# Query, output and down projections of a hybrid attention block, turned to row-wise weights and token-major results

## The chip, the cores and the metric

The kernel runs on one core of a Trainium2 chip. The metric is the device time of one launch in microseconds (us), weights read from HBM and the result written back to it. The core's engines are TensorE (PE; its weight loads are shown apart as PEld), VectorE (DVE), ScalarE (ACT), GpSimd (POOL) and SyncE (SP), which only issues transfers. All arithmetic is float32. A product is made to float32 precision from halves: each operand is split into a high part, rounded to the format fp32r that PE reads at full rate, and a low part, the rest; of the four products of halves three are added up.

## The reference

16 meta tokens go ahead of 256 tokens of 1024 channels, so L = 272. Cut to what matters here:

```python
a = rmsnorm(h, norm_mix_g)
q, k, v, qi, ki, wi, cu, cb, cc, ga, gb = split(a @ w_in)      # qi: 8 indexer heads of 64
y_attn = dsa_attention(q, k, v, qi, ki, wi) @ w_attn_out       # indexer scores -> top-k keys -> softmax
y_conv = (cb * short_conv(cc * cu, conv_w)) @ w_conv_out
h = h + (sigmoid(ga) * y_attn + sigmoid(gb) * y_conv) @ w_out
f = rmsnorm(h, norm_ffn_g)
h = h + (silu(f @ w_gate) * (f @ w_up)) @ w_down               # d_ff = 2816
out = rmsnorm(h, norm_final_g)[:, 16:]
```

## The kernel before

All activations lie channel-major: 128 channels on the partitions, tokens along the free dimension, 8 such tiles for 1024 channels. A weight matrix is cut into units of 128 x 1024 (512 KB). In a unit of the projections lie the eight 128 x 128 blocks that give 128 output channels. The list `UNITS` sets the order of all 158: four units of indexer queries (`qi`), three early gates, indexer keys (`ki`), convolution, attention, gates and branch outputs, eight of `wo`, 44 of gate and up, 22 of down. w0, w1, ... below are units by their place in that list. SP loads them in this order into seven buffers (`load_to`, line 130), ACT makes the high half (line 137), DVE the low half (line 145), some units ahead of PE (`ahead`).

PE takes the weight block as stationary operand and the activations as moving operand. `product` (lines 250, 253) needs two matmuls per block: the high weights against the high and low activations side by side (512 columns), the low weights against the high ones (256 columns). `narrow` (lines 214 to 216) needs three of 256 to 272 columns.

**Opening.** SP loads the first weight unit and the activations `h_in` in turn (lines 169, 171). The query units w0 to w3 and the early gates run on activations that carry the gain but not yet the 1/rms (`uT`, made by ACT in line 544 and DVE in line 545), one unit after the other. In between ACT squares the eight tiles of h (line 554), DVE and POOL add them up, 12 small matmuls against a column of ones sum over channels (line 191), POOL raises to the power -1/2 (line 201) and PE spreads the result (line 207), ACT copies it to `rstd` (line 590). Then POOL, ACT and DVE make the normalised activations `aT`, tile by tile (lines 563 to 565), on which unit 7 (`ki`) and all later ones run. `indexer_queries` (lines 294, 296) moves each query unit out of PSUM, in two ACT and two DVE instructions, while the next one runs.

**Joint and end.** Each of the eight `wo` units gives 128 channels of the residual; DVE adds them to h, ACT and DVE make the two halves of the FFN's input `fT` (lines 633, 634) and ACT the squares, POOL adds these. The first gate unit follows, then eight small matmuls for the sums. Gate and up run in pairs for each 128 channels of d_ff. In the down part one output tile takes 22 blocks in a row in one PSUM bank. After the last one come transposes back to token-major (line 691), the sums, the power, four evictions with the scale (lines 702, 703) and four transfers out (line 705).

Of the kernel before, what the change touches and what calls it, by code (L numbers as in the profile page):

```python
# [11 lines left out]
F32 = mybir.dt.float32  # L12
# [4 lines left out]
P = 128  # L17
# [25 lines left out]
START = [("w", 0, 4), ("h", 0, 2), ("h", 2, 4), ("w", 4, 8), ("h", 4, 6), ("h", 6, 8)]  # L43
# [22 lines left out]
LEAD = 4 + len(EARLY_GATES)  # L66


def program(nc, tc, h_in, params, weights, out):
# [94 lines left out]
    par = one.tile([P, 6 * KT], F32, name="par")  # L164
    nc.scalar.dma_start(par, params)
    raw[0] = raws.tile([P, D], F32, name="raw")
    for what, a, b in START:
        if what == "w":
            nc.sync.dma_start(raw[0][:, a * P:b * P], weights[0, :, a * P:b * P])
        else:  # L170
            nc.sync.dma_start(h_all[:, a:b], h_in[:, a:b])
    state["dma"] = 1
# [3 lines left out]
    g_mix, g_ffn, g_fin = (par[:, i * KT:i * KT + KT] for i in range(3))  # L176
    cw = par[:, 3 * KT:6 * KT]
# [9 lines left out]
    def token_sums(parts, groups, where=bank):  # L187
        o = [where() for _ in groups]
        for i, sq in enumerate(parts):
            for t, (c0, n) in enumerate(groups):  # L190
                mm(o[t][0:n, 0:1], sq[:, c0:c0 + n], ones, start=i == 0, stop=i == len(parts) - 1)
        return o

    def inverse_rms(o, groups):
        r = ring.tile([P, 3], F32, name="rt")
        if len(groups) == 3:
            V.memset(r[:, 0:1], 1.0)
        for t, (c0, n) in enumerate(groups):
            V.tensor_scalar(r[0:n, t:t + 1], o[t][0:n, 0:1], 1.0 / D, EPS, op0=OP.mult, op1=OP.add)
        r = r[:, 0:len(groups)]  # L200
        G.tensor_tensor(r, r, half[:, 0:len(groups)], OP.pow)  # L201
        return r

    def spread(r, groups):
        o = side()
# [12 lines left out]
    def narrow(i, src, c0=0, late=False):  # L218
# [4 lines left out]
        for k in range(KT):  # L223
            xh, xl = src.hi[:, k, c0:n], src.lo[:, k, c0:n]
            if late:
                mm(o, hi[:, w(k)], xh, start=k == 0, stop=False)
                mm(o, hi[:, w(k)], xl, start=False, stop=False)
            else:
                three_passes(o, hi[:, w(k)], lo[:, w(k)], xh, xl, k == 0, k == KT - 1)
        if late:  # L230
            for k in range(KT):
                mm(o, lo[:, w(k)], src.hi[:, k, c0:n], start=False, stop=k == KT - 1)
# [4 lines left out]

    def accumulate(h, o):
        V.tensor_tensor(h, h, o[:, 0:S], OP.add)  # L239
        if o.shape[1] > S:  # L240
            V.tensor_tensor(h, h, o[:, S:2 * S], OP.add)
# [12 lines left out]

    def product(i, src, c0=0):
        o = bank()
        hi, lo = got.pop(i)
        w = lambda k: slice(k * P, k * P + P)
        for k in range(KT - 1):
            wide_high(o, hi[:, w(k)], src, k, c0, start=k == 0, stop=False)  # L260
            wide_low(o, lo[:, w(k)], src, k, c0, start=False, stop=False)
        k = KT - 1
        wide_low(o, lo[:, w(k)], src, k, c0, start=False, stop=False)
        wide_high(o, hi[:, w(k)], src, k, c0, start=False, stop=True)
        return o

# [24 lines left out]
    def indexer_queries(o, j):  # L291
        rows = [(slice(e * DI, e * DI + DI), slice(DI - e * DI, P - e * DI)) for e in range(2)]
        for e, (mine, other) in enumerate(rows):
            act(qi[mine, 2 * j + e], o[mine], AF.Copy)
# [460 lines left out]
```

## Time and profile before

| | before |
|---|---|
| median of three runs | 499.12 us (498.91 to 499.23) |
| the profiled execution, its own time | 498.63 us |
| its span in the profile | 496.8 us |
| mean granted clock of PE | 0.996 |
| busy: PE, PEld, DVE, ACT, POOL | 487.0, 442.7, 362.3, 300.3, 73.4 us |
| transfers | 86.09 MB, mean 173 GB/s |

A busy PE is not PE at its peak, since matmuls overlap in the pipe: the step from one start to the next says more than the duration. The profile names lines of the kernel before; a helper's instructions all carry the helper's line.

### The profile page before, as it was taken

The page shows a single profiled execution, that of the slowest core. Times are in us where ns is not written, and L with a number is a line of the kernel's source. Part 1 is how long each engine was busy: PE and PEld are TensorE (multiplying, and loading weights), DVE is VectorE, ACT ScalarE, POOL GpSimd, SP SyncE. Part 2 cuts the span into 40 slices and gives each one's busy share as a digit, 9 for nine tenths or more (in the row PEclk, how much of TensorE's full clock was granted, in tenths as well). Part 3 has the DMA queues.
Part 4 walks back from the last instruction along what each step waited for, and adds up shares of the span by engine and source line. Part 5 has one row for each costly group of instructions (what it writes and reads, how often), then busy time and mean ns, then how long its engine had stood idle before and what let it go on. Part 6 is the DMA issues. An engine that isn't in the chain of part 4 may idle for free.

```text
span 496.8 us, 8349 instructions
## 1 busy us (share of the span) xinstructions
PE 487.0 (98%) x3157; PEld 442.7 (89%) x3157; DVE 362.3 (73%) x661; ACT 300.3 (60%) x567; POOL 73.4 (15%) x75
## 2 busy tenths in 40 slices
PE   8999999999999999999999999999999999999995
PEld 6989999999999999888888989888888888888895
DVE  4898888987777766787677796788777777664521
ACT  6685656665777776855555566566566565553511
POOL 3451113130000000000000022212211122001110
PEclk9999999999999999999999999999999999999998
DMA  8947446456443445365555465466555555655002
GB/s 304 331 136 254 136 162 206 154 194 212 149 148 128 147 155 162 102 198 181 202 188 194 136 233 184 136 205 211 178 202 172 190 192 178 219 195 171 1 0 86
DMA packets 24376, 86.09 MB, mean 173 GB/s; under 512 B 2832, under 2 KB 2832, under 8 KB 24336
## 3 DMA queue, kind: packets, MB, share of 16 engines
q1 hardware_dynamic: 24192, 85.54, 52.2%
q8 instruction: 25, 0.41, 0.4%
q14 instruction: 15, 0.12, 0.1%
q10 hardware_dynamic: 144, 0.02, 0.0%
HBM read 84.50 MB, written 1.05 MB: 172 GB/s over the span
## 4 chain that ended last, share of the span: by engine, by line
PE 90%; issue 3%; DVE 2%; ACT 1%; DMA 1%; POOL 1%; SPq 0%; POOLq 0%; DVEq 0%
PE acc L250 42%; PE acc L253 22%; PE acc L215 7%; PE acc L216 7%; PE acc L214 7%; DMA h_all<-in_h_in_dram 1%; DVE aT L565 1%; PE misc L409 1%; ACT temp L554 0%; PE misc L426 0%; PE misc L302 0%; POOL rt L201 0%; PE misc L214 0%; ACT whi L137 0%; PE misc L216 0%
## 5 line engine op out<-in xcount | busy, mean ns | idle before, releaser
L250 PE MATMUL acc<-aT,whi 128*128 128x512 f32 x576 | 202.5, 398 | 0.0
L145 DVE TENSOR_TENSOR wlo<-raw,whi 128x1024 fp32r<-128x1024 f32 x158 | 192.8, 1225 | 7.3 <-ACT whi L137 5.0
L137 ACT ACTIVATE whi<-raw 128x1024 fp32r<-128x1024 f32 x158 | 163.9, 1047 | 0.4 <-PE acc L250 0.3
L253 PE MATMUL acc<-aT,wlo 128*128 128x256 f32 x576 | 150.1, 281 | 0.0
L250 PEld LDWEIGHTS acc<-aT,whi 128*128 128x128 f32 x576 | 105.4, 188 | 19.3
L250 PE MATMUL acc<-big,whi 128*128 128x512 f32 x330 | 115.2, 394 | 0.0
L253 PEld LDWEIGHTS acc<-aT,wlo 128*128 128x128 f32 x576 | 108.9, 189 | 5.7
L253 PE MATMUL acc<-big,wlo 128*128 128x256 f32 x330 | 88.4, 282 | 0.0
L215 PE MATMUL acc<-aT,whi 128*128 128x272 f32 (+2 forms) x272 | 78.1, 287 | 1.1 <-DVE aT L565 1.1
L214 PE MATMUL acc<-aT,whi 128*128 128x272 f32 (+2 forms) x272 | 78.1, 287 | 0.0
L216 PE MATMUL acc<-aT,wlo 128*128 128x272 f32 (+2 forms) x272 | 77.6, 285 | 0.0
L246 DVE TENSOR_TENSOR temp<-acc,temp 128x256 f32<-128x256 f32 x87 | 36.9, 424 | 49.4 <-ACT temp L245 49.4
L250 PEld LDWEIGHTS acc<-big,whi 128*128 128x128 f32 x330 | 60.6, 188 | 11.9
L253 PEld LDWEIGHTS acc<-big,wlo 128*128 128x128 f32 x330 | 62.1, 188 | 2.5
L215 PEld LDWEIGHTS acc<-aT,whi 128*128 128x128 f32 x272 | 51.3, 189 | 1.8 <-DVE aT L565 1.3
L214 PEld LDWEIGHTS acc<-aT,whi 128*128 128x128 f32 x272 | 51.5, 189 | 0.1
L216 PEld LDWEIGHTS acc<-aT,wlo 128*128 128x128 f32 x272 | 51.2, 188 | 0.0
L119 ACT ACTIVATE big<-temp 128x256 fp32r<-128x256 f32 x45 | 18.8, 418 | 48.3 <-DVE temp L659 23.2
L622 POOL TENSOR_TENSOR sq_sum<-sq_sum,temp 128x256 f32<-128x256 f32 x12 | 11.0, 920 | 234.9 <-ACT temp L619 234.9
L245 ACT ACTIVATE temp<-acc 128x256 f32<-128x256 f32 x87 | 32.6, 375 | 13.8 <-PE acc L250 11.5
L655 POOL TENSOR_TENSOR temp<-temp,rstd 128x256 f32<-128x256 f32 x22 | 26.0, 1181 | 93.9 <-ACT temp L654 93.9
L239 DVE TENSOR_TENSOR h_all<-h_all,acc 128x256 f32<-128x256 f32 x16 | 6.6, 415 | 28.6 <-PE acc L250 21.7
(162 smaller groups left out, 526.0 us busy)
## 6 DMA issues: line engine op xcount, KB each, us to landing
raw<-in_weights_dram SPq DMA_DIRECT2D x158, 512.0 KB, 3.4
h_all<-in_h_in_dram SPq DMA_DIRECT2D x4, 272.0 KB, 4.5
out_dram<-big SPq DMA_DIRECT2D x4, 256.0 KB, 2.3
raw<-in_weights_dram SPq DMA_DIRECT2D x2, 256.0 KB, 4.0
par<-in_params_dram ACTq DMA_DIRECT2D x1, 24.0 KB, 3.1
```

Source lines behind the costliest of these rows:

```text
L119: act(hi, src, AF.Copy)
L137: act(high[i], raw[i], AF.Copy)
L145: V.tensor_sub(lo, raw.pop(i), high[i].bitcast(F32))
L214: mm(o, wh, xh, start=first, stop=False)
L215: mm(o, wh, xl, start=False, stop=False)
L216: mm(o, wl, xh, start=False, stop=last)
L245: act(t, o[:, S:2 * S], AF.Copy)
L246: V.tensor_tensor(t, o[:, 0:S], t, OP.add)
L250: mm(halves(o), w, src.both[:, k, :, c0:c0 + S], **kw)
L253: mm(o[:, 0:S], w, src.hi[:, k, c0:c0 + S], **kw)
L622: G.tensor_tensor(sq_sum, sq_sum, sq, OP.add)
L655: G.tensor_tensor(s, s, rstd, OP.mult)
```

## The change

The weights of `qi`, `wo` and `down` are stored by rows (`by_rows`): a unit holds 128 input channels of all 1024 (for `qi`: two times 512) output channels.

- **wo and down** take the activations, 128 tokens wide, as stationary operand and 512 (at the end of down twice 256) columns of weights as moving operand, three passes each (`by_tokens`). The results are token-major, so h is loaded a second time by rows (`h_tok`) and the residual is added there. The loop over input channels is the outer one; the last three units (`HELD`) are taken one output part after the other, so that the parts end in turn.
- **Queries.** The loop over the eight tiles of h is the outer one; four units run side by side in four PSUM banks, 12 matmuls per tile. ACT issues the transfers of h, SP those of the weights. The four units are moved out of PSUM after the first half of the next unit and after `rstd`.
- **Sums of squares** come from ACT's accumulator on token-major rows: at the start on a third copy of h (`x_all`), after `wo` and `down` on the residual. The small matmuls against ones are gone. The transposes at the end are gone; 16 of h stand between `wo` and gate (`turn`), and ACT and DVE make `fT` from their PSUM banks, two tiles to a bank (`ffn_inputs`). The first gate and the first up unit are each cut in halves of four blocks.
- **End.** The final gain is multiplied in by POOL and DVE, tile 0 is scaled and sent while tile 1 is still in the matmuls.

```diff
+def by_rows(w):
+    n = w.shape[1]
+    return w.reshape(-1, D // n, P, n).transpose(0, 2, 1, 3).reshape(-1, P, D)
+    def by_tokens(o, hi, lo, src, k, t, c, first, last):
+        x = slice(t * P, t * P + P)
+        mm(o, src.hi[:, k, x], hi[:, c], start=first, stop=False)
+        mm(o, src.hi[:, k, x], lo[:, c], start=False, stop=False)
+        mm(o, src.lo[:, k, x], hi[:, c], start=False, stop=last)
...
+    for k in range(2):
+        nc.sync.dma_start(raw[0][:, k * 512:k * 512 + 512], weights[0, :, k * 512:k * 512 + 512])
+        nc.scalar.dma_start(h_all[:, k:k + 1], h_in[:, k:k + 1])
+    for i in range(1, QI):
+        nc.sync.dma_start(raw[i], weights[i])
+        nc.scalar.dma_start(h_all[:, 2 * i:2 * i + 2], h_in[:, 2 * i:2 * i + 2])
...
+    for k in range(KT):
+        act(uT.hi[:, k], hT[:, k], AF.Copy, scale=g_mix[:, k:k + 1])
+        V.tensor_copy(high[i][:, c], raw[i][:, c])
+        (G if k < KT - 2 else V).tensor_tensor(low[:, c], raw[i][:, c], high[i][:, c].bitcast(F32), OP.subtract)
+        V.scalar_tensor_tensor(uT.lo[:, k], hT[:, k], g_mix[:, k:k + 1], uT.hi[:, k].bitcast(F32),
+                               op0=OP.mult, op1=OP.subtract)
+        for j in range(QI):
+            mm(queries[j][:, 0:S], high[i][:, w[j]], uT.hi[:, k], start=k == 0, stop=False)
...
+    def mean_square(col, rows, t):
+        act(x_all[rows, t], x_all[rows, t], AF.Square, scale=D ** -0.5, accum_out=mean[rows, col:col + 1])
+    def all_rms():
+        act(rstd, spread(mean, ALL)[:, 0:L], AF.Copy)
...
+            o = narrow(i, uT, midway=all_rms)
+            for j in range(QI):
+                indexer_queries(queries[j], j)
...
+    def residual(o, t, c, col):
+        V.tensor_tensor(h_tok[:, t, c], h_tok[:, t, c], o, OP.add)
+        return lambda: act(o, h_tok[:, t, c], AF.Square, scale=D ** -0.5, accum_out=sums[:, t, col:col + 1])
+    def ffn_inputs(n):
+        for j in range(n * KT // 2, (n + 1) * KT // 2):
+            src = turned_h[j // 2][:, (j % 2) * S:(j % 2) * S + S]
+            act(fT.hi[:, j], src, AF.Copy, scale=g_ffn[:, j:j + 1])
+            V.scalar_tensor_tensor(fT.lo[:, j], src, g_ffn[:, j:j + 1], fT.hi[:, j].bitcast(F32),
+                                   op0=OP.mult, op1=OP.subtract)
...
+    for place, ((t, n), o) in enumerate(outs.items()):
+        for k in range(KT - HELD, KT):
+            by_tokens(o, hi, lo, mixed, k, t, QUARTERS[n], False, k == KT - 1)
+        square = residual(o, t, QUARTERS[n], n)
+        if place == 1:
+            turn(0, 0)
+        if place == 2:
+            turn(1, 0)
+            ffn_inputs(0)
...
+        blocks(*opening[u], fT, lower, 0, True, False)
+        if u == 0:
+            turn(0, 1)
+            turn(1, 1)
+            ffn_inputs(1)
+            square()
+            V.scalar_tensor_tensor(r, sums[:, :, 0], EPS, sums[:, :, 1], op0=OP.add, op1=OP.add)
+            inverse_rms(r)
...
+    PARTS = [(0, 0, 512), (0, 512, D), (1, 0, 512), (1, 512, 768), (1, 768, D)]
+    def finish(t):
+        y = scaled[t]
+        for n, c in QUARTERS.items():
+            if n == 0:
+                act(y[:, c], y[:, c], AF.Copy, scale=r[:, t:t + 1])
+                nc.scalar.dma_start(out[t * P:t * P + P, c], y[:, c])
+            else:
+                V.tensor_scalar(y[:, c], y[:, c], r[:, t:t + 1], None, op0=OP.mult)
+                nc.sync.dma_start(out[t * P:t * P + P, c], y[:, c])
...
+        residual(outs[part], t, c, part % 2 if t == 0 else part - 2)()
+        (V if c1 - c0 < 512 else G).tensor_tensor(scaled[t][:, c], h_tok[:, t, c], g_fin[:, c], OP.mult)
+        if part in (1, 4):
+            inverse_rms(r[:, t:t + 1])
+            finish(t)
```

Three places of the instruction order follow. Names in brackets are semaphores that the instruction waits for; DMAHW0 to DMAHW7 are the eight that transfers share in turn.

ACT at the start of the program, before:

```order
L159 ACTIVATE temp<-ones 128x1 [waits DVE_49]
L165 DMA par<-in_params_dram 128x48
L544 ACTIVATE big_135<-h_all,par 128x256 [waits DMAHW3_49,DMAHW1_49]
L544 ACTIVATE big_135<-h_all,par 128x256
L544 ACTIVATE big_135<-h_all,par 128x256 [waits DMAHW2_49]
```

and after (DMAHW0 is at that point the first half of w0, DMAHW2 is w1):

```order
L166 DMA par<-in_params_dram 128x40
L171 DMA h_all<-in_h_in_dram 128x272 x2
L174 DMA h_all<-in_h_in_dram 128x544
L174 DMA h_all<-in_h_in_dram 128x544 [waits DMAHW0_49]
L174 DMA h_all<-in_h_in_dram 128x544 [waits DMAHW2_49]
L535 ACTIVATE big_139<-h_all,par 128x256 [waits DMAHW4_49,DMAHW3_49]
L535 ACTIVATE big_139<-h_all,par 128x256 [waits DMAHW5_49]
```

Five issues of h have moved from SP to ACT and stand ahead of ACT's first product (L535, L544 before).

DVE around the 1/rms, before (L199 makes the mean squares, L296 moves queries out, L145 splits a weight unit, L565 makes `aT`, L570 an early gate):

```order
L199 TENSOR_SCALAR rt<-misc 16x1
L199 TENSOR_SCALAR rt<-misc 128x1 x2
L145 TENSOR_TENSOR wlo<-raw,whi 128x1024
L296 TENSOR_TENSOR big_122<-acc,big_122 64x256 x2
L145 TENSOR_TENSOR wlo<-raw,whi 128x1024
L296 TENSOR_TENSOR big_122<-acc,big_122 64x256 x2
L565 SCALAR_TENSOR_TENSOR aT<-temp,par,aT 128x272 x2
```

and after (L579, L290, L146, L558 and L563 in the same roles):

```order
L579 TENSOR_SCALAR rt<-rt 128x3
L146 TENSOR_TENSOR wlo<-raw,whi 128x1024
L290 TENSOR_TENSOR big_127<-misc,big_127 64x256 x8
L146 TENSOR_TENSOR wlo<-raw,whi 128x1024
L558 SCALAR_TENSOR_TENSOR aT<-temp,par,aT 128x272 x2
L563 TENSOR_TENSOR gate_392<-acc,rstd 128x256
L146 TENSOR_TENSOR wlo<-raw,whi 128x1024
L558 SCALAR_TENSOR_TENSOR aT<-temp,par,aT 128x272 x3
```

Of the four pairs of L296 only two stood after L199; now all four stand after it, ahead of the split of w6 (the second L146).

ACT between `wo` and gate, before (L633 makes the high half of `fT`, L619 the squares, L137 splits weights):

```order
L633 ACTIVATE aT<-h_all,par 128x256 [waits DVE_49]
L619 ACTIVATE temp<-h_all 128x256
```

and after (L628 makes the high half of `fT`, L613 the squares):

```order
L613 ACTIVATE misc,sums<-h_all 128x512 [waits DVE_49] x2
L628 ACTIVATE aT<-acc,par 128x256 [waits PE_49]
L628 ACTIVATE aT<-acc,par 128x256 [waits DVE_49]
L613 ACTIVATE misc,sums<-h_all 128x512
L628 ACTIVATE aT<-misc,par 128x256 [waits PE_49]
L628 ACTIVATE aT<-misc,par 128x256 [waits DVE_49]
L613 ACTIVATE misc,sums<-h_all 128x512
L138 ACTIVATE whi<-raw 128x1024 [waits DMAHW4_49,Activation_49]
```

L628 stands eight times, alternately behind PE and behind DVE; before, its input was h in SBUF.

## Rows read from the trace of the kernel before

**Rows 1.** The page's part 4: the chain that ended last, by engine:

```profile
PE 90%; issue 3%; DVE 2%; ACT 1%; DMA 1%; POOL 1%; SPq 0%; POOLq 0%; DVEq 0%
```

**Rows 2.** A stage: its us, busy PE to POOL (x), clock, DMA share, GB/s:

```profile
34.00:273.00 239.00, 238.41 (x1657) 222.75 (x1658) 185.95 (x385) 156.45 (x322) 17.38 (x18) 1.00 0.53 172
```

**Rows 3.** The chain in order of time: start, us, two down outputs' first matmuls:

```profile
426.48 0.47 PE acc L250 x2
434.22 0.46 PE acc L250 x2
```

**Rows 4.** The timeline of PE in the opening: start, us, what, [idle before]:

```profile
5.46 0.47 PE L226 MATMUL acc<-big,whi 128*128 128x256 f32 x1
...
6.22 0.28 PE L226 MATMUL acc<-big,whi 128*128 128x256 f32 x1
...
6.62 0.28 PE L226 MATMUL acc<-big,whi 128*128 128x256 f32 x1
...
10.57 1.11 PE L232 MATMUL acc<-big,wlo 128*128 128x256 f32 x8
...
22.34 0.59 PE L207 MATMUL misc<-ident,rt 16*128 16x16 f32 x3 [0.65 <-POOL rt L201]
...
34.59 0.39 PE L215 MATMUL acc<-aT,whi 128*128 128x272 f32 x1 [1.11 <-DVE aT L565]
```

**Rows 5.** The timeline of ACT in the opening:

```profile
4.64 1.75 ACT L544 ACTIVATE big<-h_all,par 128x256 fp32r<-128x256 f32 x4 [2.42 <-DMA h_all<-in_h_in_dram]
...
22.96 0.40 ACT L590 ACTIVATE rstd<-misc 128x272 f32<-128x272 f32 x1 [3.64 <-PE misc L207]
...
24.20 0.75 ACT L294 ACTIVATE big<-acc 64x256 fp32r<-64x256 f32 x2
```

**Rows 6.** Waits of SP's queue up to 20 us: total, times, longest:

```profile
SPq L130 <- DMA h_all<-in_h_in_dram: 1.0, 3, 0.5
```

**Rows 7.** The same table, four stretches of the opening:

```profile
2.00:4.00 2.00, 2.00 (x6) 1.55 (x6) 0.11 (x1) 0.22 (x2) 0.00 (x0) 1.00 0.89 293
4.00:6.00 2.00, 1.93 (x8) 1.36 (x6) 1.13 (x3) 1.36 (x4) 1.27 (x1) 1.00 1.01 283
6.00:8.00 2.00, 1.57 (x7) 1.08 (x7) 1.48 (x4) 0.59 (x2) 0.45 (x1) 1.00 0.98 359
14.00:16.00 2.00, 2.00 (x19) 2.00 (x18) 1.92 (x4) 2.00 (x5) 1.57 (x2) 1.00 1.03 414
```

**Rows 8.** The timeline of POOL in the opening:

```profile
4.40 1.27 POOL L541 TENSOR_TENSOR wlo<-raw,whi 128x512 fp32r<-128x512 f32 x1 [2.85 <-DVE whi L540]
...
20.39 1.89 POOL L201 TENSOR_TENSOR rt<-rt,half 128x3 f32<-128x3 f32 x1 [4.49 <-DVE rt L199]
23.44 8.50 POOL L563 TENSOR_TENSOR temp<-h_all,rstd 128x272 f32<-128x272 f32 x8 [1.15 <-ACT rstd L590]
```

**Rows 9.** The timeline of DVE in the opening:

```profile
24.40 1.64 DVE L145 TENSOR_TENSOR wlo<-raw,whi 128x1024 fp32r<-128x1024 f32 x1 [1.94 <-POOL temp L563]
26.07 0.86 DVE L296 TENSOR_TENSOR big<-acc,big 64x256 fp32r<-64x256 f32 x2
...
34.05 1.31 DVE L565 SCALAR_TENSOR_TENSOR aT<-temp,par,aT 128x272 fp32r<-128x272 f32 x3
```

**Rows 10.** The timelines of ACT, DVE and PE at the joint:

```profile
302.70 0.51 ACT L633 ACTIVATE aT<-h_all,par 128x256 fp32r<-128x256 f32 x1 [0.58 <-DVE h_all L239]
...
303.24 0.48 DVE L634 SCALAR_TENSOR_TENSOR aT<-h_all,par,aT 128x256 fp32r<-128x256 f32 x1 [0.58 <-ACT aT L633]
...
304.17 0.50 PE L191 MATMUL acc<-ones,sq_sum 128*128 128x1 f32 x4
```

**Rows 11.** The timelines of PE, POOL and SP's queue at the end:

```profile
488.42 1.03 PE L691 MATMUL misc<-ident,h_all 128*128 128x128 f32 x8
...
490.51 0.71 POOL L201 TENSOR_TENSOR rt<-rt,half 128x2 f32<-128x2 f32 x1 [7.46 <-DVE rt L199]
...
491.97 1.82 SPq L705 DMA_DIRECT2D out_dram<-big  x4
```

More of the change, by code (lines that the diff above doesn't have):

```diff
@@ L185, in program, with inverse_rms @@
     B = [(0, P), (P, P)]
[L187 to L202, printed above, removed]
+    def inverse_rms(r):
+        G.tensor_tensor(r, r, half[:, 0:r.shape[1]], OP.pow)
     def spread(r, groups):
-        o = side()
+        o = bank()
         for i, (c0, n) in enumerate(groups):
@@ L223, in narrow @@
         for k in range(KT):
+            if midway and k == KT // 2:
+                midway()
             xh, xl = src.hi[:, k, c0:n], src.lo[:, k, c0:n]
[L225 to L232, printed above, removed]
+            three_passes(o, hi[:, w(k)], lo[:, w(k)], xh, xl, k == 0, k == KT - 1)
         return o
@@ L253, in wide_low, with blocks @@
         mm(o[:, 0:S], w, src.hi[:, k, c0:c0 + S], **kw)
+    def blocks(o, hi, lo, src, ks, c0, first, last):
+        w = lambda k: slice(k * P, k * P + P)
+        for k in ks:
+            end = last and k == ks[-1]
+            if not end:
+                wide_high(o, hi[:, w(k)], src, k, c0, start=first and k == ks[0], stop=False)
+            wide_low(o, lo[:, w(k)], src, k, c0, start=False, stop=False)
+            if end:
+                wide_high(o, hi[:, w(k)], src, k, c0, start=False, stop=True)
     def product(i, src, c0=0):
@@ L624, in final_rms @@
-    def final_rms():
-        return inverse_rms(token_sums([sq_sum, sq_last], B), B)
-    for j in range(KT):
-        i = first["wo"] + j
-        ahead(i)
-        o = product(i, mix()) if j < KT - 1 else narrow(i, mix())
-        h = hT[:, j]
-        accumulate(h, o)
-        act(fT.hi[:, j], h, AF.Copy, scale=g_ffn[:, j:j + 1])
-        pending.append(lambda j=j, h=h: V.scalar_tensor_tensor(
-            fT.lo[:, j], h, g_ffn[:, j:j + 1], fT.hi[:, j].bitcast(F32), op0=OP.mult, op1=OP.subtract))
-        if j == KT - 1:
-            flush()
-        sq_last = squares(j, h)
+    sums = one.tile([P, 2, 4], F32, name="sums")
@@ L640, in program @@
     gu = [Twin(one, S, f"big{b}") for b in range(3)]
     rstd = rstd[:, 0:S]
+    r = ring.tile([P, 3], F32, name="rt")[:, 0:2]
+    opening = {}
+    gate = first["gate"]
+    lower, upper = range(KT // 2), range(KT // 2, KT)
+    for u in range(2):
+        opening[u] = (bank(), *got.pop(gate + u))
+        blocks(*opening[u], fT, lower, 0, True, False)
[3 more added lines that the diff above has]
+            ffn_inputs(1)
+            square()
+            V.scalar_tensor_tensor(r, sums[:, :, 0], EPS, sums[:, :, 1], op0=OP.add, op1=OP.add)
+            inverse_rms(r)
@@ L643, in program @@
+    for u in range(2):
+        blocks(*opening[u], fT, upper, 0, False, True)
     for j in range(NF):
-        i = first["gate"] + 2 * j
+        i = gate + 2 * j
         ahead(i)
-        og = product(i, fT)
         if j == 0:
-            r = final_rms()
-            ahead(i + 1)
-            ou = product(i + 1, fT)
+            og, ou = opening[0][0], opening[1][0]
             act(rstd, spread(r, B)[:, 0:S], AF.Copy)
+        else:
+            og = product(i, fT)
         s = total(og)
@@ new lines, in program, with down_block @@
+    flush()
+    PARTS = [(0, 0, 512), (0, 512, D), (1, 0, 512), (1, 512, 768), (1, 768, D)]
+    outs = [side() for _ in range(4)] + [bank()]
+    outs = [o[:, 0:c1 - c0] for o, (t, c0, c1) in zip(outs, PARTS)]
+    def down_block(k, part, hi, lo):
+        t, c0, c1 = PARTS[part]
+        by_tokens(outs[part], hi, lo, gu[k // KT], k % KT, t, slice(c0, c1), k == 0, k == NF - 1)
+    for k in range(NF - HELD):
+        ahead(down + k)
+        for part in range(len(PARTS)):
+            down_block(k, part, *got[down + k])
+        got.pop(down + k)
+        if k == NF - HELD - 3:
+            scaled = [raws.tile([P, D], F32, name="raw") for _ in range(2)]
+            g_fin = raws.tile([P, D], F32, name="raw")
+            nc.sync.dma_start(g_fin, gains)
```

231 lines of the change are left out of this document (95 added, 136 removed).

## The prediction

> **What bounds the kernel now.** Read the chain of waits first: TensorE is 90% of it [rows 1]. Then the table by stage: from 34 to 273 us PE is busy 238.41 of 239.00 us [rows 2]. So in the body nothing that another engine saves is worth anything, and what a stage costs there is its PE time. Time can move in three places only: the opening (0 to 35.8 us, where PE starts late, waits, and at last runs dry on the normalised input), the joint between output projection and FFN, and the end after the last matmul. A fourth term is the speed of the rewritten matmul streams.
>
> **The streams (wo, down).** The columns stay the same: a weight unit was eight pairs of 512 + 256 and is now 12 x 512 (wo) or 9 x 512 and 6 x 256 (down), 6144 each way. The spacing has to be split into a part per column and a part per matmul. One down output, 22 pairs, takes 434.22 - 426.48 = 7.74 us, so 0.352 for a pair [rows 3]; eight 256-wide ones take 1.11 us, of which the last is 0.28, so 0.1186 each [rows 4]. Solved: 0.446 ns a column and 4.5 ns a matmul, which gives 0.233 for a 512; two 512s in a row do stand at 0.47 and 0.46 [rows 3]. wo goes from 136 to 96 matmuls and down from 374 to 330: 84 x 4.5 ns = **-0.4 us**. Bounds: 0, and -6 us (first rival).
>
> **The opening.** *When PE starts.* Before, ACT makes its first product at 4.64 us [rows 5] and the first query matmul stands at 5.46 [rows 4]. After, ACT itself issues the h transfers and they stand ahead of its products in its queue. The order shows that the fourth waits for the first half of w0 and the fifth for w1, because transfers share eight completion semaphores. That such waits bind is seen on SP before: 1.0 us in three waits behind h transfers [rows 6]. So ACT cannot make even product 0 before w1 has landed. Ahead of that lie w0 and w1 (1.05 MB) on SP and, interleaved, 0.56 to 0.83 MB of h on ACT: 1.6 to 1.9 MB. The early windows move 2 x (0.293 + 0.283) = 1.15 MB by 6 us and 1.87 MB by 8 us [rows 7], so w1 lands at about 8 (5.5 if SP's queue were served alone, 9 with a landing delay of 1). Then the last h issue and a product: first query matmul at about 8.9, 3.4 late.
>
> *How long the queries take.* The 96 query matmuls are as many as before. At the start PE ran with a spacing of (6.62 - 6.22)/2 = 0.20 [rows 4], the 1.2 GHz level, and at 10.57 with 0.119, the 2.4 GHz level, although the granted clock reads 1.00 all along [rows 4, 7]; five us of query matmuls went before. I take four us at 0.20 again (20 matmuls), then 76 x 0.1186 = 9.0: queries done at 21.9. The inner loop has cover: per k step PE needs 1.42 us, POOL 1.27 for the low half [rows 8], DVE a cast and a product of about 0.45 each.
>
> *RMS.* Before, twelve small matmuls and a chain through DVE and POOL gave the spread at 22.34 [rows 4]. After, ACT accumulates from rows that land when 4.8 MB are in; at 0.414 MB per us after 8 us [rows 7] that is 15 to 16 us. Three ACT squares at about 1.25, an addition that stands behind DVE's query work, and a POOL power of 1.89 [rows 8] end between 20.5 and 22.7. The spread stands midway in unit 4, behind 12 matmuls: 21.9 + 1.4 = 23.3. PE, not the sums, sets it: **+1.0** against 22.34 (bounds -2.1 and +3).
>
> *From the scale to the normalised input.* Before: scale at 22.96 + 0.40 = 23.36 [rows 5], last product at 34.05 + 1.31 = 35.36 [rows 9], 12.0 us, bound by DVE. Six of eight query evictions were done by then. After, all eight pairs stand behind the scale, as the order shows. ACT needs 4 x 0.75 = 3.0 [rows 5] and DVE, 0.43 each [rows 9], is through at 0.8 + 3.45 = 4.25 after the scale; the split of w6 follows (1.64 while POOL works [rows 8, 9]) and ends at 5.9, where before it and its pair ended at 26.93, 3.57 after. That is 2.3 late. Part returns, since POOL's eight products end 8.6 after the scale [rows 8] and DVE then runs undisturbed (three products in 1.31 [rows 9]). In us after the scale: two products, disturbed, to 7.6, a gate 8.0, w7 9.4, three products 10.7, a gate 11.1, w8 12.3, three products 13.6, instead of 12.0: **+1.6** (bounds 0 and +2.6). PE will wait for w6 and then, longer than the 1.11 us of now [rows 4], in unit 7. Sum of the opening: **+2.6**.
>
> **The joint.** Before, the gate product follows the last wo unit without a gap; its last input is needed only at its end. Then come eight small matmuls of the sums, about 0.1 apart (the first four take 0.50 with the last one's tail [rows 10]): -0.8. After, 16 transposes stand here; eight take 1.03, the last of it 0.28, so 0.107 each [rows 11]: +1.7. The wait is new: the inputs of a half come from PSUM, two to a bank, and the order shows that ACT's second read of a bank waits for DVE, so ACT (about 0.47; 0.51 from SBUF [rows 10]) and DVE (0.48 [rows 10]) take turns. Four inputs need 3.7 us. First half: transposes end 0.4 into place 3 (2.1 us of PE), the fourth input at 4.2, wanted at 3.6: 0.6 of wait. Second half: DVE adds the last residual only after the first four inputs; transposes are done 5.4 in, the inputs at 9.1, and PE, which has 1.41 us of the up unit as cover, wants the eighth at 7.9: 1.15. Behind that the sum, a POOL power under a DVE split (the 1.64 kind) and the spread: 0.3 of wait. Joint: 1.7 - 0.8 + 1.75 + 0.3 = **+3.0**. Bounds: +0.9 with no wait, +4.5 if each turn takes half as long again.
>
> **The end.** Before, 8.4 us from the last matmul (488.42) to the end: transposes, sums, a power (0.71 [rows 11]), four evictions and four transfers, issued from 491.97 for 1.82 us, so the last from 493.3, 4.9 after PE's end [rows 11]. After: no transposes, half the output already leaving. But DVE scales the first half (waiting for the power of tile 0) ahead of the third residual, and ACT issues a transfer there. By DVE's order, in us after PE's end and with durations scaled from those of 256 columns: the 512-wide residual of tile 1 ends at 0.0, the 256-wide one at 0.4, its multiply at 1.2, the partial sum (it waits for ACT's squares) at 1.65, the last residual at 2.05, its square with the read of the accumulator at 2.7, the power at 3.66, the scaling at 4.35, the issue starts at 4.4: **-0.6** (bounds -1.8 with the first scaling out of the way, +0.5). Elsewhere the change costs nothing: h rows and gains (1.5 MB) go in a stretch where DMA is at 0.53 [rows 2], and the sums move off POOL, which is idle.
>
> **Sum.** 2.6 + 3.0 - 0.6 - 0.4 = +4.6 us. The profiled execution has 498.63 (span 496.8), 0.49 below the median of the three runs; I add the sum to the median, 499.12: **503.7**. All bounds at one side give 490 and 510; they won't fall together. About 0.2% (1 us) can be told from no change.
>
> **Rivals.** *The wide stream is faster.* 768 columns at the 2.4 GHz level are 0.320, the rows show 0.352. If the surplus belongs to weight loads that a 512-wide matmul covers fully, the 294 wide ones of wo and down fall from 0.233 to 0.2133: -5.7, and the time is 498.4: not slower. It decides from a spacing of 0.216 on. For it: every 512 before alternates with a 256. Against: the two 512s in a row. The Trainium skill (TensorE: Matmul & The Clock Gate, Back-to-back issue gap) gives columns at 2.4 GHz plus 2.5 ns for one matmul, 0.2158 for 512; by that the sum would be about -0.1 instead of +4.6. The trace differs: 0.233. Chance 0.16.
>
> *The second queue delivers early.* If w1 lands by 5.5, PE starts at 6, is at 2.4 GHz by 10, the spread comes near 20.2 when the sums allow it, 2.1 early; with the evictions' 1.6 the opening gains 0.5, and if ACT and DVE hide in the joint (+0.9) and the end gains 1.0, the time is 498.1, and 497.3 if the end gains its full 1.8. For it: two sequencers issue. Against: the transfer engines are at 0.89 to 1.01 already from 2 to 6 us [rows 7]. Chance 0.20.
>
> *PE stays at 1.2 GHz through the queries,* because it stands idle longer ahead of them than now: the 76 matmuls at 0.20 instead of 0.1186 cost 6.2 more: 509.9. For it: the low level outlasted five us of matmuls before [rows 4]. Against: it did end. Chance 0.06.
>
> **How the numbers follow.** Forecast 503.7, chance 0.58, own range 500.5 to 507. The rivals at 498.4 and 498.1 are split over faster, same and slower (0.10, 0.06, 0.00; 0.10, 0.04, 0.06). Faster 0.20, same 0.10, slower 0.70. Range 497.8 to 507.6: below it lies about half of the faster share, above it the last rival and a little of the forecast's own spread.
>
> **What would show it.** PE's first query matmul near 8.9 and ACT's first product right after w1; the spread near 23.3; the last normalised product near 38; a wait of PE at unit 6; in the joint two waits of PE on DVE of 0.6 and 1.2; the last issue near 4.4 after PE's end. Wrong if ACT's first product comes before 6, if 512-wide matmuls stand below 0.22 apart, or if ACT's second reads overlap DVE's.

## The result: 5.3 us slower, through the opening and the joint

The changed kernel takes **504.28 us** (median; 504.13 to 504.39) against **499.01 us** (498.82 to 499.23) of the kernel before: ratio 1.0105, 95% interval [1.0088, 1.0123]. That is 5.3 us slower, where 4.6 was forecast. The profiled execution took 504.19 with a span of 502.4, 5.6 over the span before (496.8).

The 5.6 can be laid out by stage, because PE has the same landmarks in both traces. Three of them in the trace of before: the first matmul of the output projection, the first of the FFN, and the spread behind the first gate and up product (start, us, what).

```profile
278.93 0.39 PE L250 MATMUL acc<-big,whi 128*128 128x512 f32 x1
...
301.39 0.39 PE L250 MATMUL acc<-aT,whi 128*128 128x512 f32 x1
...
307.89 0.38 PE L207 MATMUL misc<-ident,rt 128*128 128x128 f32 x2
```

The same three in the trace of after (the FFN is L234 now, the spread L201), with the last matmul:

```profile
283.19 0.40 PE L257 MATMUL misc<-whi,big 128*128 128x512 f32 x1
...
306.47 0.39 PE L234 MATMUL acc<-aT,whi 128*128 128x512 f32 x1
...
314.39 0.38 PE L201 MATMUL acc<-ident,rt 128*128 128x128 f32 x2
...
494.95 0.28 PE L259 MATMUL acc<-whi,big 128*128 128x256 f32 x1
```

| stage | before, us | after, us | difference | forecast |
|---|---|---|---|---|
| start to the end of PE's wait in unit 7 | 34.59 [rows 4] | 38.77 | +4.18 | +2.6 |
| body, to the first output projection matmul | 244.34 | 244.42 | +0.08 | 0 |
| output projection and joint, to the spread | 28.96 | 31.20 | +2.24 | +3.0, less a part of the streams' 0.4 |
| FFN and down, to the end of PE's last matmul (488.42 [rows 11]; 494.95 + 0.12) | 180.53 | 180.68 | +0.15 | the rest of the -0.4 |
| end of the last matmul to the end of the span | 8.38 | 7.33 | -1.05 | -0.6 |

### The profile page after: what moved, and what is told of

The parts are those of the page before. It is cut to its first block, busy times and chain, and to the rows that moved or that the text cites. A ratio compares the mean times of both kernels' runs of the same rounds, so it can differ in the third digit from the quotient of the medians.

```text
span 502.4 us, 8096 instructions
## 1 busy us (share of the span) xinstructions
PE 486.1 (97%) x3045; PEld 436.1 (87%) x3045; DVE 357.1 (71%) x642; ACT 294.6 (59%) x556; POOL 66.8 (13%) x68
## 3 DMA queue, kind: packets, MB, share of 16 engines
HBM read 87.18 MB, written 1.05 MB: 176 GB/s over the span
## 4 chain that ended last, share of the span: by engine, by line
PE 89%; DVE 4%; issue 3%; ACT 2%; DMA 1%; POOL 1%; SPq 0%; POOLq 0%; ACTq 0%
PE acc L234 32%; PE acc L237 16%; PE acc L209 7%; PE acc L210 7%; PE acc L208 7%; PE misc L259 5%; PE misc L257 5%; PE misc L258 5%; DMA raw<-in_weights_dram 1%; DVE whi L536 1%; DVE aT L629 1%; DVE aT L558 1%; ACT big L288 1%; ACT aT L628 1%; DVE wlo L146 1%
## 5 line engine op out<-in xcount | busy, mean ns | idle before, releaser
L146 DVE TENSOR_TENSOR wlo<-raw,whi 128x1024 fp32r<-128x1024 f32 x155 | 188.2, 1220 | 27.7 <-PE acc L258 20.6
L234 PE MATMUL acc<-aT,whi 128*128 128x512 f32 x576 | 203.1, 399 | 0.5 <-DVE aT L629 0.3
L138 ACT ACTIVATE whi<-raw 128x1024 fp32r<-128x1024 f32 x155 | 161.6, 1049 | 27.7 <-PE acc L259 22.7
L234 PEld LDWEIGHTS acc<-aT,whi 128*128 128x128 f32 x576 | 105.1, 188 | 20.8 <-DVE aT L629 1.3
L257 PE MATMUL misc<-whi,big 128*128 128x512 f32 (+1 forms) x120 | 45.1, 376 | 0.0
L259 PE MATMUL misc<-whi,big 128*128 128x512 f32 (+1 forms) x120 | 45.0, 375 | 0.0
L258 PE MATMUL misc<-wlo,big 128*128 128x512 f32 (+1 forms) x120 | 44.8, 373 | 0.0
L234 PE MATMUL acc<-big,whi 128*128 128x512 f32 x120 | 42.3, 396 | 0.0
L237 PE MATMUL acc<-big,wlo 128*128 128x256 f32 x120 | 31.3, 281 | 0.0
L196 POOL TENSOR_TENSOR rt<-rt,half 128x1 f32<-128x1 f32 (+2 forms) x4 | 2.7, 672 | 204.7 <-DVE rt L670 196.7
```

What stands on the lines that cost most here:

```text
L138: act(high[i], raw[i], AF.Copy)
L146: V.tensor_sub(lo, raw.pop(i), high[i].bitcast(F32))
L234: mm(halves(o), w, src.both[:, k, :, c0:c0 + S], **kw)
L237: mm(o[:, 0:S], w, src.hi[:, k, c0:c0 + S], **kw)
L257: mm(o, src.hi[:, k, x], hi[:, c], start=first, stop=False)
L258: mm(o, src.hi[:, k, x], lo[:, c], start=False, stop=False)
```

## The profile after

The chain of waits (page, part 4: shares of the span) has little more of the other engines in it than before [rows 1], and a stage of 239 us in the body is as full as it was [rows 2] (columns as there):

```profile
PE 89%; DVE 4%; issue 3%; ACT 2%; DMA 1%; POOL 1%; SPq 0%; POOLq 0%; ACTq 0%
```

```profile
38.00:277.00 239.00, 238.23 (x1655) 222.12 (x1656) 185.90 (x385) 155.90 (x321) 17.41 (x18) 1.00 0.55 176
```

The opening on PE (start, us, what, [idle before, who ended it]), to be read against [rows 4]. PE starts 3.1 late (its second group of four shows the pace of that start, 0.213 a matmul), the spread comes 3.2 late, and it waits on POOL's power for 1.78; then PE waits for w6 (0.98) and in unit 7 (1.08):

```profile
8.53 1.22 PE L542 MATMUL misc<-big,whi 128*128 128x256 f32 x4 [2.87 <-ACT big L535]
9.55 1.05 PE L544 MATMUL misc<-big,whi 128*128 128x256 f32 x4
...
25.53 0.59 PE L201 MATMUL acc<-ident,rt 16*128 16x16 f32 x3 [1.78 <-POOL rt L196]
...
32.20 0.39 PE L210 MATMUL acc<-big,wlo 128*128 128x256 f32 x1 [0.98 <-DVE wlo L146]
...
38.77 0.39 PE L209 MATMUL acc<-aT,whi 128*128 128x272 f32 x1 [1.08 <-DVE aT L558]
```

ACT in the opening, against [rows 5]. Its h issues end at 7.86, and its first product comes right after w1. Then it stands idle for 5.29 until DVE has set the accumulators' target; only then do the three squares run, and the scale comes at 26.15 instead of 22.96:

```profile
2.28 5.58 ACTq L174 DMA_DIRECT2D h_all<-in_h_in_dram  x3
7.97 0.91 ACT L535 ACTIVATE big<-h_all,par 128x256 fp32r<-128x256 f32 x2 [5.74 <-DMA raw<-in_weights_dram]
...
21.10 1.06 ACT L570 ACTIVATE big<-big 128x1024 f32<-128x1024 f32 x1 [5.29 <-DVE rt L567]
...
26.15 0.40 ACT L573 ACTIVATE rstd<-acc 128x272 f32<-128x272 f32 x1 [0.88 <-PE acc L201]
```

DVE shows why that comes so late. The cast of half a weight unit takes 1.50 while POOL computes a low half (1.46 for one of those), and 0.42 once POOL is through; the memset (L567) is written behind all of it:

```profile
9.64 1.50 DVE L536 CAST whi<-raw 128x512 fp32r<-128x512 f32 x1
...
19.50 0.42 DVE L536 CAST whi<-raw 128x512 fp32r<-128x512 f32 x1
...
20.99 0.06 DVE L567 MEMSET rt<- 128x3 f32 x1
...
27.23 3.47 DVE L290 TENSOR_TENSOR big<-misc,big 64x256 fp32r<-64x256 f32 x8 [0.70 <-ACT big L288]
```

At the joint ACT and DVE take turns over the FFN's inputs, as forecast: each of them reads two inputs in a row only where these lie in different banks ("x2"), and waits 0.55 for the other one in between:

```profile
304.36 0.47 ACT L628 ACTIVATE aT<-acc,par 128x256 fp32r<-128x256 f32 x1 [1.31 <-PE acc L623]
305.39 0.84 ACT L628 ACTIVATE aT<-acc,par 128x256 fp32r<-128x256 f32 x2 [0.55 <-DVE aT L629]
```

At the end the last issue starts 4.0 after PE's last matmul (495.07) instead of 4.9 [rows 11]. A multiplication of 256 columns takes 1.34 on DVE while POOL does its own:

```profile
495.21 1.34 DVE L730 TENSOR_TENSOR raw<-h_all,raw 128x256 f32<-128x256 f32 x1
...
499.10 0.35 ACTq L719 DMA_DIRECT2D out_dram<-raw  x1
```

## The experiments

The theory: the opening is the time of the scale plus a fixed chain, the scale is late because the sums of squares wait for DVE, and the rest of the loss is the joint's turn-taking. Times are medians, ratios are to the kernel before on the same chip. That took 498.55 beside the memset, SyncE, low-halves and banks runs, 499.06 beside the control, all three, the old opening and all mended, and 499.38 beside the other four, so the ratios are what to compare. The opening itself varies from execution to execution: in unaltered openings of the changed kernel the scale stood at 26.15 twice, 26.84 and 27.14. The six runs with a single edit (memset, SyncE, fewer transfers, low halves, banks, end) have ratios whose intervals overlap with the control's. What such an edit did is therefore read from the landmarks of its own stage.

**The changed kernel again,** as a control: 504.14, ratio 1.0100 [1.0085, 1.0115].

> The changed kernel itself, unaltered, beside the next three on the same chip, so that they are compared with it and not with a run of another hour. Expected 5.3 us over the kernel before (ratio 1.009 to 1.012), scale at 26 to 27, the wait in unit 7 ending 12.6 after it.

Its clock tells more than its time (table by stretch, granted clock third from the end):

```profile
12.00:14.00 2.00, 2.00 (x11) 2.00 (x11) 2.00 (x3) 0.68 (x3) 1.64 (x2) 0.50 1.04 421
```

The granted clock is 0.50, the 1.2 GHz level, from 8 to 14 us, where the first profile had 1.00 from 12 on. The scale stands at 26.15 all the same: PE's speed in the queries did not set it, the sums did.

**The memset first.** 503.27, ratio 1.0092 [1.0077, 1.0107].

```diff
+    mean = ring.tile([P, 3], F32, name="rt")
+    V.memset(mean, 1.0)
     warm(WARM)
```

> The changed kernel with one line moved: the memset of the accumulators' target (rt) is written ahead of the query loop instead of behind it, everything else the same. Theory (the opening lost its time because ACT's squares of sums wait for that memset, which stands behind DVE's query work until 21.0): the squares start when ACT is free and the rows have landed, 16 to 17 us, and end by 20.3; DVE's addition, which stands behind a split, comes at 22.2; the spread is then PE's own at about 23.5 instead of 25.53, all that follows is 2 us early, time about 502.3. Rival A (the rows land late and the memset hides behind them): squares still at 20 to 21, time 504.3. Rival B (the scale is not what holds unit 7, PE's late start is): spread at 23.5, but the wait in unit 7 grows by as much and the time stays within 0.5 of 504.3.

The timelines of ACT and PE:

```profile
16.31 1.04 ACT L569 ACTIVATE big<-big 128x1024 f32<-128x1024 f32 x1
...
24.51 0.59 PE L201 MATMUL acc<-ident,rt 16*128 16x16 f32 x3
```

The squares start 4.8 earlier and PE waits for nothing at the spread. It comes at 24.51 and not at 23.5, because PE, now the bound, ran its queries at the 1.2 GHz level until past 14 us (granted clock 0.50 from 8 to 14 us). The wait in unit 7 ends at 37.74, again 12.6 after the scale (25.13).

**h issued by SyncE.** 502.62, ratio 1.0080 [1.0063, 1.0097].

```diff
-        nc.scalar.dma_start(h_all[:, k:k + 1], h_in[:, k:k + 1])
+        nc.sync.dma_start(h_all[:, k:k + 1], h_in[:, k:k + 1])
```

(and the same for the pairs of blocks behind it)

> The changed kernel with the five h transfers issued by SyncE, between the weight transfers, instead of by ACT; nothing else is changed. Theory (ACT's first product stood behind its own transfer issues, which waited for w1): first product near 4.5 instead of 7.97, first query matmul at 5 to 5.5 instead of 8.53; the DVE and POOL loop of 1.83 per k step then ends near 17.7 instead of 21.0, the memset and the squares move with it, spread at 22 to 22.5 instead of 25.53; time about 501.0. Rival A (one queue issues too slowly, so w1 to w3 or the rows come late): first matmul early, but the loop ends at 20 or later, time 503 to 504. Rival B (TensorE stays longer at its 1.2 GHz level when it starts early): queries end no earlier than 21, but the sums set the spread anyway, time 501 to 502.

```profile
4.17 0.51 ACT L535 ACTIVATE big<-h_all,par 128x256 fp32r<-128x256 f32 x1 [1.93 <-DMA h_all<-in_h_in_dram]
...
6.00 0.83 PE L542 MATMUL misc<-big,whi 128*128 128x256 f32 x4
...
23.63 0.59 PE L201 MATMUL acc<-ident,rt 16*128 16x16 f32 x3 [1.77 <-POOL rt L196]
```

ACT and PE start as the theory has it. No idle stretch lies between the warm-up matmuls and the queries here, and PE's granted clock stays at 1.00. But the loop of DVE and POOL ends at 19.1 instead of 17.7, since the second block of h landed only at 7.4; the spread gains 1.9 instead of 3. The result lies between the theory and rival A.

**Fewer h transfers, still from ACT.** 504.14, ratio 1.0099 [1.0082, 1.0116].

```diff
+        if i == 1:
+            nc.scalar.dma_start(h_all[:, 2:KT], h_in[:, 2:KT])
```

> The changed kernel with the h transfers still issued by ACT, but three instead of five (block 0, block 1, and blocks 2 to 7 in one), so that none of them has to wait for a completion of an earlier transfer; nothing else is changed. Theory (it was the shared completions, not the engine that issues, that held ACT until w1 had landed): ACT's issues end by 3, its first product comes at 4 to 4.6, the first query matmul at 5 to 6 without a low stretch of TensorE's clock, the scale near 24.3 and the time near 502.5, as with SyncE issuing. Rival A (two queues delay h itself): first product at 7 or later, 504. Rival B (blocks 2 to 7 in one transfer come so late that the loop ends no earlier than 21): first product early, scale at 26, 504.

```profile
5.75 0.51 ACT L536 ACTIVATE big<-h_all,par 128x256 fp32r<-128x256 f32 x1 [3.53 <-DMA h_all<-in_h_in_dram]
...
11.31 2.51 ACT L536 ACTIVATE big<-h_all,par 128x256 fp32r<-128x256 f32 x6 [2.75 <-DMA h_all<-in_h_in_dram]
```

ACT's issues are through at 2.74 and no product waits for w1: it was the shared completions that held ACT. The gain is spent elsewhere. h0 lands 1.6 later than from SyncE's queue, blocks 2 to 7 only at 11.3, and the scale stands at 25.84. This is rival B.

**Low halves on DVE.** 503.12, ratio 1.0089 [1.0074, 1.0104].

```diff
-        (G if k < KT - 2 else V).tensor_tensor(low[:, c], ...
+        V.tensor_tensor(low[:, c], ...
```

> The changed kernel with the six low halves of the query weights that POOL computed given to DVE, which already computed the last two; nothing else is changed. Theory (DVE's cast takes 1.50 instead of 0.42 because POOL works on the same kind of operands at that time): the casts are back at 0.42, a k step on DVE takes 1.46 as its last two did, DVE is through near 19.1 instead of 21.0, the spread comes at about 23.7, time about 502.4. Rival (the cast is long because transfers are landing in memory at that time, or because of its place): the casts stay at 1.50, a k step takes 2.6, DVE is through near 28, time about 510.

```profile
10.99 0.42 DVE L536 CAST whi<-raw 128x512 fp32r<-128x512 f32 x1
11.45 0.69 DVE L537 TENSOR_TENSOR wlo<-raw,whi 128x512 fp32r<-128x512 f32 x1
```

All eight casts take 0.42 to 0.43, in the same stretch of landing transfers: it was POOL. DVE with all the work is through at 19.8, with POOL's help at 21.0. The Trainium skill (SBUF — State Buffer, Who interferes with whom) says that DVE and GpSimd share one pair of ports by an exclusive lock. The trace of the changed kernel agrees for the cast: POOL's subtraction stands from 9.41 to 10.86, the cast from 9.64 to 11.14, so it ends 0.28 after POOL, as if it had waited for most of that. The product on DVE takes 0.47, as alone, but it starts before POOL's subtraction does (9.25 against 9.41).

**All three.** 500.11, ratio 1.0020 [1.0010, 1.0029].

> The changed kernel with all three edits of the opening at once: the memset ahead of the query loop, the h transfers issued by SyncE, the low halves on DVE. Theory (the opening ends 12.6 us after the scale, and the scale is set by the later of PE's query work and the sums; all three edits attack both): first query matmul at about 6, then PE alone paces with 1.44 per k step, queries done at 18.5 to 19, the squares at 16 to 19 lie beside it, spread at 20 to 20.5, scale near 20.8, the wait in unit 7 ends at 33.4 instead of 38.77; time 5 us below the changed kernel, 499.0 to 499.5. Rival A (the three are one and the same gain, about 1.9 in all): time near 502. Rival B (with the sums out of the way TensorE stays at its 1.2 GHz level or the rows land late, and the scale comes at 22 to 23, where it was before the change): 501.

```profile
20.86 0.22 PE L201 MATMUL acc<-ident,rt 16*128 16x16 f32 x1 [0.84 <-POOL rt L196]
...
34.13 0.40 PE L209 MATMUL acc<-aT,whi 128*128 128x272 f32 x1 [1.09 <-DVE aT L560]
```

The queries are done at 18.4, the scale stands at 21.49 and the wait ends 12.64 behind it. Singly the three edits brought the scale forward by 1.0 (memset), 1.9 (SyncE) and 1.2 (low halves), together they bring 4.7: they add up, and a little more. In the medians it is 4.0 us. The opening is now 0.5 shorter than that of the kernel before. The scale is still 0.7 later than the theory had it, since PE waited 1.21 for a product of h at 9.55 and 0.84 for POOL at the spread, and the time is 0.6 over the theory's range.

**The old opening.** 500.39, ratio 1.0024 [1.0012, 1.0036]. The diff is the opening's part of the change taken back. The query weights are still read in the changed layout, so the queries that this kernel computes are others; their amount is the same.

> The opening of the kernel before (queries unit by unit, sums by matmuls with ones, one query eviction behind the scale) put into the changed kernel; output projection, FFN, down projection and end as changed. Theory (of the loss 4.2 is the opening's, +2.3 the joint's, -1.0 the end's, +0.2 the streams'): the scale is back at 23, the wait in unit 7 ends near 34.6, time 1.0 to 1.6 us over the kernel before, ratio 1.002 to 1.0035. Rival (the opening's loss is caught up in the body anyway, or the body of the changed kernel is itself slower): 2.5 us or more over the kernel before.

```profile
23.90 0.40 ACT L612 ACTIVATE rstd<-acc 128x272 f32<-128x272 f32 x1 [4.07 <-PE acc L212]
...
35.50 0.40 PE L220 MATMUL acc<-aT,whi 128*128 128x272 f32 x1 [0.98 <-DVE aT L587]
```

The time is 1.3 us over the kernel before, as the theory has it: against the control, 3.75 of the loss is the opening's, the rest that of joint, streams and end. The chain behind the scale is 11.60 long again, as before (34.59 - 22.96 = 11.63 [rows 4, 5]). The scale itself is 0.9 later than in the kernel before; the profiled execution is the slowest of this kernel's six (501.11), and PE's granted clock was 0.50 in it from 11 to 14 us, where the profile before had 1.00.

**Banks in turn.** 503.48, ratio 1.0096 [1.0081, 1.0112].

```diff
+    HALVES = [0, 2, 1, 3], [4, 6, 5, 7]
-        for j in range(n * KT // 2, (n + 1) * KT // 2):
+        for j in HALVES[n]:
-    lower, upper = range(KT // 2), range(KT // 2, KT)
+    lower, upper = HALVES
```

> The changed kernel with the inputs of the FFN read from PSUM in the order 0, 2, 1, 3 and 4, 6, 5, 7 instead of 0 to 7 (and the matmuls that use them in the same order), so that ACT's next read is of the other bank; nothing else is changed. Theory (ACT and DVE take turns since ACT may not read a bank that DVE has still to read): four inputs take about 2.4 us instead of 3.4, PE's 16 pairs and 8 transposes between the last output projection matmul and the spread take 6.5 to 6.7 instead of 7.92; time about 502.9. Rival (the turns come from something else, or DVE's residual of the third part sets the first half): 7.9 us as before and 504.3.

The timelines of DVE, ACT and PE at the joint:

```profile
305.80 1.90 DVE L630 SCALAR_TENSOR_TENSOR aT<-acc,par,aT 128x256 fp32r<-128x256 f32 x4
...
305.29 0.84 ACT L629 ACTIVATE aT<-acc,par 128x256 fp32r<-128x256 f32 x2 [1.31 <-PE acc L624]
306.32 0.87 ACT L629 ACTIVATE aT<-acc,par 128x256 fp32r<-128x256 f32 x2 [0.19 <-DVE aT L630]
...
307.41 0.39 PE L234 MATMUL acc<-aT,whi 128*128 128x512 f32 x1
...
313.94 0.39 PE L201 MATMUL acc<-ident,rt 128*128 128x128 f32 x2
```

DVE's four inputs run without a gap, and from the first FFN matmul to the spread it is 6.53 instead of 7.92. The whole time doesn't show these 1.39: the profiled execution's scale came at 27.14, 0.99 late, which is the variation told of above, and the median's ratio can't be told from the control's. The run with all edits has the 6.53 again.

**The end reordered.** 504.04, ratio 1.0089 [1.0071, 1.0106]. The last two blocks' multiplications are moved behind the last residual.

> The changed kernel with one edit at the end: the multiplications by the gain of the last two blocks are written behind the last residual instead of between the residuals. Theory (the last residual, its square, the power and the scaling stand behind a multiplication on DVE that takes 1.34 beside GpSimd's, 0.42 when alone): the last issue ends 3.5 after the last matmul starts instead of 4.5, time 0.6 to 0.7 below the changed kernel, about 503.5. Rival (what comes last is the landing of the output, and it takes its time from the first half's transfers): the last issue comes earlier, but the span still ends 7.3 to 7.5 after the last matmul, 504.1.

```profile
495.67 0.28 PE L259 MATMUL acc<-whi,big 128*128 128x256 f32 x1
...
499.12 0.35 ACTq L719 DMA_DIRECT2D out_dram<-raw  x1
```

The last issue comes 3.45 after the last matmul's start where the changed kernel has 4.15, and the span ends 6.8 after it instead of 7.45: that is the theory, in its stage. In the whole time 0.6 can't be told from the opening's variation (scale at 26.84 here): by the medians the run is inconclusive.

**All mended.** 497.63, ratio 0.9972 [0.9960, 0.9983]: 6.5 us below the changed kernel, and faster than the kernel before.

```diff
     inverse_rms(mean)
+    indexer_queries(queries[0], 0)
     split_to(QI + 2)
```

(with the edits of the opening, the banks and the end)

> The three edits of the opening, one of the four query units evicted ahead of the scale, the FFN inputs read with the banks in turn, and at the end the multiplications by the gain of the last two blocks written behind their residuals. Theory: opening as in the run with the three edits, less 0.9 for the two evictions (the wait in unit 7 ends 11.7 after the scale), joint 6.5 instead of 7.9 from the last output projection matmul to the spread, end 6.4 instead of 7.3 from the last matmul to the end of the span (the last residual no longer stands behind a multiplication that takes 1.34 beside GpSimd); in sum 3 us below the run with the three edits, 496 to 496.5, under the kernel before by 0.5%. Rival (ACT's two evictions and its split push the scale back by as much, and GpSimd's power stands behind its own multiplication at the end): only the joint's 1.4 is gained, 497.6 to 498.

```profile
21.68 8.82 POOL L558 TENSOR_TENSOR temp<-h_all,rstd 128x272 f32<-128x272 f32 x8 [1.15 <-ACT rstd L572]
...
488.32 0.28 PE L259 MATMUL acc<-whi,big 128*128 128x256 f32 x1
...
491.79 0.34 ACTq L720 DMA_DIRECT2D out_dram<-raw  x1
```

The joint is 6.53 and the last issue 3.47 behind the last matmul, as wanted. The early eviction brought 0.3 instead of 0.9 (the chain is 12.35), while POOL's products take 8.82 instead of 7.11. That DVE's splits beside them are the reason is not shown by a run of its own. The time is the one that the rival named, but not for its reasons: the end did gain, 0.6 against the run with the three edits, and the scale came 0.3 earlier than there. The span still ends 7.28 after the last matmul's start, only 0.2 sooner than in the changed kernel, because more time lies behind the last issue (see the last section).

**Evictions last,** in the kernel with the three edits (501.02, ratio 1.0034 [1.0021, 1.0047]) and in the mended one (499.23, ratio 1.0002 [0.9992, 1.0012]).

```diff
     early_gate(o, LEAD - 1)
+    for j in range(QI):
+        indexer_queries(queries[j], j)
```

> The kernel with the three edits of the opening, and the eight query evictions of ACT and of DVE written behind the normalised products and the gates instead of ahead of them; they are wanted only later, by the scores. Theory (the 12.6 from the scale to the end of the wait in unit 7, 11.6 before the change, is a chain on DVE that begins with 3.47 of query evictions): the chain falls to 9.2 to 10, GpSimd's products then set it (7.1 to 8.8 for eight), PE's waits for w6 and for the normalised input (1.3 and 1.1) are gone; time 2 to 2.5 below the run with the three edits, about 497.8. Rival (the evictions, moved behind, hold up DVE's splits for units 8 to 10, and PE waits there): 0.5 or less is gained, 499.6 or more.

> The three edits of the opening, the query evictions behind the normalised products, the FFN inputs with the banks in turn, the end reordered: all that the runs so far speak for. Theory (the gains lie in three separate places and add up): 2 us under the run with all of that but one early eviction (497.63), 495.5 to 496. Rival (PE becomes the bound in the opening, the waits were partly one another's cover): 497 or more.

PE in the first of the two:

```profile
32.60 0.40 PE L209 MATMUL acc<-aT,whi 128*128 128x272 f32 x1 [1.23 <-DVE aT L560]
...
38.50 0.39 PE L210 MATMUL acc<-aT,wlo 128*128 128x258 f32 x1 [1.44 <-DVE wlo L146]
...
42.12 0.28 PE L282 MATMUL misc<-ident,temp 8*128 8x8 f32 x2 [0.72 <-DVE temp L275]
```

Both were expected to gain. By the ratios they lost 0.7 against the run with the three edits, where the intervals overlap, and 1.5 against the mended one, which has one eviction early; this second loss is clear of the noise. The chain behind the scale fell to 11.4 only (POOL's products took 8.71), and in the first run two new waits of 1.44 and 0.72 came behind it, as its rival had it. The evictions cost DVE 3.47 in the new place too.

## Why the prediction was right, and where its steps were not

The sum of 4.6 stands close to 5.3 because errors cancelled, which is luck in part. Measured by the profile's 5.6, the opening was 1.6 too low and the streams 0.4, the joint was 0.7 and the end 0.45 too high, and 0.2 came in units that the change left as they were.

**The opening.** The first step held: the first product waits for w1 (7.97), the first query matmul stands at 8.53 for 8.9, the queries are done at 22.15 for 21.9. But one reading under it was wrong. The spacing of 0.20 at the start of the kernel before was not the 1.2 GHz level, as the granted clock of 1.00 says [rows 7]. PE waited there for DVE's products, of which the last three start 0.40 apart, and each is good for two matmuls:

```profile
5.19 1.95 DVE L545 SCALAR_TENSOR_TENSOR big<-h_all,par,big 128x256 fp32r<-128x256 f32 x4 [0.87 <-ACT big L544]
```

In the changed kernel the low level did come (0.50 from 8 to 11 us, 0.213 a matmul), behind an idle stretch of 2.87 that the kernel before doesn't have. So the four us at 0.20 came true by luck. The same reading was what spoke for the third rival.

The step that failed is "PE, not the sums, sets it". It rested on the inner loop's cover, with DVE's cast and product at 0.45 each. Beside POOL the cast takes 1.50, a k step 1.83, and DVE is through at 21.0. The squares themselves cost 1.05 each where 1.25 was put, but the memset that they wait for stands in DVE's queue, and that was not followed. The spread lost 3.2 instead of 1.0. The step behind the scale had the right mechanism and the wrong size: 12.62 against 11.63, +1.0 for +1.6. The wait for w6 (0.98) and the one in unit 7 (1.08) came where they were forecast, the latter no longer than before.

**The joint.** Right mechanism, smaller size. The matmul behind four transposes stands 0.32 from the next one instead of 0.23, so four cost PE 0.35 and then 0.09 more:

```profile
301.41 0.60 PE L623 MATMUL acc<-ident,h_all 128*128 128x128 f32 x4
301.76 0.48 PE L257 MATMUL misc<-whi,big 128*128 128x512 f32 x1
302.08 0.40 PE L258 MATMUL misc<-wlo,big 128*128 128x512 f32 x1
302.31 0.39 PE L259 MATMUL misc<-whi,big 128*128 128x512 f32 x1
```

Counted so, the 16 transposes cost 1.75 (0.44, 0.44 and 0.87) for 1.7, and the sums by matmul that are gone 0.9 for 0.8. The waits are the rest of the 7.92 from the first FFN matmul to the spread: 7.05 without the transposes, against 5.60 before without the sums (6.50), so 1.45 for 1.75. About 0.4 of it lies in the first half and 1.0 in the second, for 0.6 and 1.15. The spread waits for nothing, where 0.3 had been added. That is 2.3 for 3.0. Banks in turn took back 1.39 of the 1.45.

**The streams.** The 512 stands at 0.233, as worked out (302.08 to 302.31 above), and the first rival (0.216 or less) is out. But the 4.5 ns that each matmul less was to save hardly show. The output projection without its transposes took 22.40 (23.28 less 0.88) where it had taken 22.46. The down part's first matmul, before and after:

```profile
426.56 0.40 PE L250 MATMUL acc<-big,whi 128*128 128x512 f32 x1
```

```profile
433.18 0.39 PE L257 MATMUL misc<-whi,big 128*128 128x512 f32 x1
```

From there to the end of PE's last matmul it is 61.86 before and 61.89 after. Together that is -0.03 instead of -0.4, at the edge of the bounds. In the output projection one reason can be seen: the last unit of before ran as 24 matmuls of 256 columns that stand 0.113 apart, not 0.1186. Why the down part saved nothing stays open. The other 0.12 of the stage stand in gate and up units. The Trainium skill (TensorE: Matmul & The Clock Gate, Back-to-back issue gap) would have 0.2158 for one 512 by itself; this trace shows 0.233 in a stream.

**The end.** -1.05 for -0.6: the issue starts 4.0 after PE's last matmul, not 4.4. What was missed on the other side is the multiplication beside POOL, 1.34 instead of 0.42; without it the stage would have gained 0.6 more, as the reordered end shows.

**The rivals.** The second queue did not deliver early (7.97). The 1.2 GHz level did last through a good part of the queries in the control (to 14 us), and cost nothing there, because the sums were later.

## What to carry to other kernels

Before an engine is given a small new job, follow its place in that engine's queue: a memset of 0.06 us, written behind 12 us of other work, held up the whole opening by 1.0 us. Count an operation's duration from a row in which the same neighbours are at work, and treat a chain with a fixed length behind one event (here 12.6 us behind the scale, in nine profiles) as the thing to shorten at its start. Where two engines read pairs of tiles from one bank, let the order of reads alternate the banks.

## What the runs showed of the hardware that was not expected

- A DVE cast of 128x512 takes 0.42 alone and 1.50 beside a POOL subtraction of the same size, which itself goes from 1.26 to 1.46; a DVE multiplication of 128x256 goes from 0.42 to 1.34.
- In the six profiles in which PE stood idle for 2.7 to 3.2 us between the warm-up matmuls and the queries, its granted clock fell to 0.50 afterwards and stayed there for 3 to 7 us, in the same program for different lengths. In seven without that stretch it stayed at 1.00. With the old opening it was 0.50 from 11 to 14 us although PE had waited no longer than 1.02 us at a time since the warm-up, so that stretch is not the only way to the low level.
- From the end of the last output issue the span lasts 3.4 to 3.5 us in the five changed kernels in which SyncE issues h, 3.0 to 3.1 in those with h issued by ACT. It is no rule of the issuer: with the old opening it is 3.2, in the kernel before 3.0, and in both SyncE issues h too. What makes the 0.4 was not found.
